# Longer assumed latencies between DVE or ACT and the small products, in an instruction order made by a planner

## The chip, the cores and the metric

The kernel runs on one core of one Trainium2 chip. The metric is the device time of one execution in microseconds (us), as a median of several executions; lower is better. The engines are called as in the profile: PE (matrix products), DVE (vector), ACT (scalar), POOL (GpSimd) and SP (issues of DMA transfers).

## What is computed

Two residual layers on x of 2048 positions by 1024 channels, all in float32. The first layer's mixer is a gated linear recurrence, the second a gated delta rule with 8 heads of 128 by 128. Cut to what matters here:

```
h = rmsnorm(x) * (1 + scale_c) + shift_c                      # c: conditioning
# layer 0: RG-LRU
xb, zg = split(h @ in_w);  xb = causal_conv4(xb) + b
r, i   = sigmoid(blockdiag(gate_w) @ xb + gate_b)             # 8 blocks of 128 x 128
a      = exp(-8 * r * softplus(-lam))
y_t    = a_t * y_{t-1} + sqrt(1 - a_t^2) * i_t * xb_t
x      = x + gate_c * ((y * silu(zg)) @ out_w)
# layer 1: gated delta rule, per head
q, k, v = silu(causal_conv4(h @ in_w));  q, k normalized
S_t = a_t S_{t-1} + beta_t k_t (v_t - a_t S_{t-1}^T k_t)^T;   o_t = S_t^T q_t
x   = x + gate_c * ((rmsnorm(o) * silu(z)) @ out_w)
return rmsnorm(x) * final_g
```

## The kernel before: five stages, and a planner that writes the order

**Stages.** PE's long work is in four projections of 128x512 products on f32r operands, all issued at L670: each float32 operand is split into a high and a low part, and each product is made of three (high by high, high by low, low by high), 24 products for one panel of 128 channels and one tile of 512 positions. In the order in which they run: the input projection of layer 0 for the first and the second half of the sequence (32 jobs of 24 products each half), its output projection, the input projection of layer 1 for the first and the second half (64 jobs each), its output projection. I call these products the main products.

**Small products between them.** In layer 0 each tile of a channel block passes from PE to ACT (L730, a copy), POOL (L744, the first tap), DVE (L718, three taps), ACT (L768, the high part `xh`) and DVE (L771, the low part `xl`), and then returns to PE for the two gates: six products `pg` at L777, of which the second reads `xl`. In layer 1 the tiles of k, q and v come from DVE at L978. From k, PE makes transposes `pk` (L1090) and the Gram blocks `pkk` (L1125), from q and k the blocks `pqk` (L1210). The inverse of a triangular matrix is built for each head: 62 short instructions on DVE for its 32x32 blocks (L1245, L1248, with `blk`, `tblk` and `ttmp`), and three levels that merge blocks with four groups of small products, `px` (L1287), `pr` (L1299, L1302), `px` (L1316) and `pr` (L1326), each of which waits for ACT or DVE to bring back the one before. Then the recurrence of the head runs over 8 chunks of 128 positions for each half of the sequence. One chunk is a closed chain:

- PE `pp` (L1365, L1366): state by k and by q
- DVE `zt` (L1374)
- PE `py` (L1382)
- ACT `yt` (L1388)
- PE `pS` (L1394, L1395)
- DVE: the new state (L1407), which the next `pp` reads.

**The order.** Nothing is ordered on the chip except by each engine's own queue and by semaphores. The queues are written by a planner (class `Weave`) that runs when the program is built. Each piece of work is a generator; it says which engine it wants and for how long, and optionally what latency follows until a reader on another engine can start. The planner always takes the thread that can start first:

```
            else:
                self.free[w[0]] = t + w[1]
                th.t = t + w[1] + (w[2] if len(w) > 2 else self.LAG[w[0]])
```

Here `w[0]` is the engine, `w[1]` the assumed duration, and `w[2]` the assumed latency; without it the latency is `LAG`, 0.3 for DVE and ACT. A reader can thus not be placed before the assumed duration and latency are over, and the planner fills PE with main products meanwhile. Buffers are counted slots: a thread that asks for one of them stops until an earlier holder gives it back. The ones that matter here are those of layer 1: `kt` has 6 and `qt` 5 tiles (`KTN, QTN`), `ac`, `atn`, `kd` and `vn` have 4, and each head uses two of each for a half of the sequence. A job of main products for k or q asks for its `kt` or `qt` tile before its first product, and the recurrence gives one back after the `pp` of every fourth chunk. The thread that issues main products works through its jobs one after the other, so a job that waits for a tile holds up all main products.

Of the kernel before, what the change touches and what calls it, by code (L numbers as in the profile page):

```python
# [31 lines left out]
BLK = 2  # L32
KTN, QTN = 6, 5
EPS = 1e-6

# [103 lines left out]
def trunk_kernel(ctx, tc, x, c, ada_w, ada_b, ada_c, norm_c, final_g, w1, cw1, cb1, gate_w, gate_b, lam, ow1,  # L139
                 w2, wab, cw2, a_log, dt_bias, onorm, ow2, out):  # L140
    nc = tc.nc
    act, dve, pool, pe, sp = nc.scalar, nc.vector, nc.gpsimd, nc.tensor, nc.sync
# [616 lines left out]
    def gates_thread(u, n, i):  # L759
# [8 lines left out]
        act.copy(xh, xf)  # L768
        yield "dve", EV
        xl = tile_([P, TC], "xr", "xl", F32R)  # L770
# [181 lines left out]
    def conv2_thread(u, kind, h, i, pt, mtok, rtok):  # L952
# [21 lines left out]
        if kind == "v":  # L974
            rtok = yield slots["vt"]
        yield "dve", EV
        r = tile_([P, TC], kind + "t", kind + "t")
# [282 lines left out]
    def levels_thread(u, h):  # L1260
# [15 lines left out]
        for b in range(3):  # L1276
            for i in range(NTC):
                yield "dve", 0.2, 0.0 if b < 2 or i == 0 else 0.27
                o = 32 * (b % 2)
                dve.transpose(out=tf[32 * b:32 * b + 32, i, :, o:o + 32],  # L1280
                              in_=acs[i][32 * b:32 * b + 32, :, 32 * b:32 * b + 32])
# [8 lines left out]
        act.activation(tf[32:64, :, :, 0:32], px[32:64], AF.Copy, scale=-1.0)  # L1290
        yield "dve", 0.33
        dve.tensor_scalar(tf[96:128, :, :, 0:32], px[96:128], -1.0, None, ALU.mult)
# [15 lines left out]
        for i, a in ((0, 0), (1, 0), (1, 64)):  # L1308
            yield "dve", 0.2, 0.27 if a else 0.0
            dve.tensor_copy(out=acs[i][a:a + 32, :, a + 32:a + 64], in_=pr[a:a + 32, 0, i])  # L1310
# [7 lines left out]
        act.activation(tf[64:128, 0], px[64:128, 0], AF.Copy, scale=-1.0)  # L1318
        yield "dve", 0.33
        dve.tensor_scalar(tf[64:128, 1], px[64:128, 1], -1.0, None, ALU.mult)  # L1320
# [19 lines left out]
    def recurrence_thread(u, h):  # L1340
# [4 lines left out]
        for i in range(NTC):  # L1345
# [7 lines left out]
            for b in range(TB):  # L1353
# [16 lines left out]
                if not first:  # L1370
                    ztok = yield slots["zt"]
                    yield "dve", 0.27
                    zt = tile_([P, P], "zt", "zt")
                    dve.scalar_tensor_tensor(zt, pp[:, 0, :], eg[:, 0, m, h:h + 1], vn[:, b, :], ALU.mult,  # L1374
                                             ALU.subtract)
                    hold.done()
# [8 lines left out]
                ytok = yield slots["yt"]  # L1385
                yield "act", 0.16
                yt = tile_([P, P], "yt", "yt")
# [13 lines left out]
                if last:  # L1401
                    return
                yield "dve", 0.27
                if first:
# [334 lines left out]
```

## Time and profile before

| | |
|---|---|
| median of three runs | 1983.85 us (1979.78 to 1991.28) |
| time of the profiled execution | 1989.06 us |
| its span, first to last instruction | 1987.3 us, granted clock of PE 0.981 |
| busy | PE 1869.0, DVE 1500.0, ACT 1025.1, POOL 811.3 us |

The profile gives, for each instruction, its engine, line, start and duration, and for an engine's idle time the instruction elsewhere that ended it. A duration of PE overlaps with that of the next product, so PE's pace is read from the distance of two starts and not from the mean duration. Lines of a view of waits read: engine and line that waited, `<-` what it waited for, us in total, times, longest.

### The profile page before, as it was taken

To read this page: it belongs to the slowest core of one execution; us is meant where nothing else is said; L and a number is where in the kernel's file an instruction comes from. 1 tells how busy PE (TensorE), PEld (TensorE's weight loads), DVE (VectorE), ACT (ScalarE), POOL (GpSimd) and SP (SyncE) were. 2 spreads that over 40 slices of the span, in tenths; PEclk is the share of its full clock that TensorE was granted. 3 is DMA by queue.
4 is the path that set the end of the run, shared out by engine and by line. 5 is a ranking of instruction groups with operands and counts; after the bars stand their busy time and mean duration, and the time that the engine had idled before them with its cause. 6 is when DMAs were issued, how large, how long until landed. Compare 5 with 4: busy or idle time off the path is not lost.

```text
span 1987.3 us, 31679 instructions
## 1 busy us (share of the span) xinstructions
PE 1869.0 (94%) x10408; PEld 1520.6 (77%) x10408; DVE 1500.0 (75%) x3176; ACT 1025.1 (52%) x2453; POOL 811.3 (41%) x1439
## 2 busy tenths in 40 slices
PE   6998889999999999999998989999999999999998
PEld 3776667787787777777777777788888888878887
DVE  6788798887644566888888897778777778877654
ACT  3655567666411225455555655555655556655321
POOL 4555664444200146555555553364343335511101
PEclk9999999999999999999999999999999999999999
DMA  8355655654578724546764447455455445577751
GB/s 333 97 159 160 220 169 171 199 170 156 172 199 206 223 63 127 136 111 160 177 161 126 107 115 187 135 125 146 114 129 142 120 127 128 142 208 233 224 185 64
DMA packets 506957, 314.33 MB, mean 158 GB/s; under 512 B 370724, under 2 KB 438564, under 8 KB 506792
## 3 DMA queue, kind: packets, MB, share of 16 engines
q1 hardware_dynamic: 506792, 312.31, 55.5%
q8 instruction: 82, 1.34, 0.3%
q14 instruction: 83, 0.68, 0.1%
HBM read 211.54 MB, written 100.67 MB: 157 GB/s over the span
## 4 chain that ended last, share of the span: by engine, by line
PE 50%; DVE 20%; DMA 10%; POOL 6%; issue 5%; ACT 5%; SPq 4%; DVEq 0%; POOLq 0%; ACTq 0%
PE mm L670 25%; PE mmo L670 12%; DVE xf L718 5%; DVE tblk L1248 2%; DVE ttmp L1245 2%; PE pg L777 2%; SPq L515 1%; DMA raw<-in_w 1%; DMA pq<-q_d 1%; DVE acc L415 1%; PE pp L1365 1%; PE py L1382 1%; DMA ada<-in_ada_w 1%; PE pS L1394 1%; PE pS L1395 1%
## 5 line engine op out<-in xcount | busy, mean ns | idle before, releaser
L718 DVE SCALAR_TENSOR_TENSOR xf<-xe,cw_s,xf 128x512 f32<-128x512 f32 x384 | 327.8, 855 | 54.9 <-POOL xf L961 32.0
L652 POOL TENSOR_TENSOR wlo<-raw,whi 128x1024 fp32r<-128x1024 f32 x48 | 122.3, 2548 | 81.0 <-ACT whi L646 67.9
L733 POOL COPY carry<-xe 128x4 f32<-128x4 f32 x128 | 36.8, 287 | 249.3 <-ACT xe L730 248.4
L1245 DVE TENSOR_TENSOR ttmp<-blk,tblk 128x60 f32<-128x60 f32 (+24 forms) x496 | 121.9, 246 | 21.0 <-DMA blk<-blk_d 11.0
L1248 DVE TENSOR_TENSOR tblk<-tblk,ttmp 128x60 f32<-128x60 f32 (+24 forms) x496 | 127.3, 257 | 10.1
L646 ACT CAST whi<-raw 128x1024 fp32r<-128x1024 f32 x96 | 100.3, 1045 | 52.8 <-DMA raw<-in_w 43.5
L730 ACT COPY xe<-mm 128x512 f32<-128x512 f32 x128 | 74.1, 580 | 78.6 <-PE mm L670 77.8
L670 PE MATMUL mmo<-oh,yh 128*128 128x512 f32 x256 | 102.2, 399 | 7.3 <-DVE xr L925 6.2
L670 PE MATMUL mm<-hh_('in2', 0)_5430,wlo 128*128 128x512 f32 x256 | 105.1, 411 | 0.0
L670 PE MATMUL mm<-hl_('in2', 0)_5431,whi 128*128 128x512 f32 x256 | 105.1, 410 | 0.0
L670 PE MATMUL mm<-hl_('in2', 1)_12333,whi 128*128 128x512 f32 x256 | 104.8, 409 | 0.0
L670 PE MATMUL mm<-hh_('in2', 0)_5430,whi 128*128 128x512 f32 x256 | 104.4, 408 | 0.0
L670 PE MATMUL mm<-hh_('in2', 1)_12332,wlo 128*128 128x512 f32 x256 | 104.3, 408 | 0.0
L670 PE MATMUL mm<-hh_('in2', 1)_12512,wlo 128*128 128x512 f32 x256 | 104.1, 407 | 0.0
L670 PE MATMUL mm<-hl_('in2', 0)_5208,whi 128*128 128x512 f32 x256 | 103.6, 405 | 0.0
L670 PE MATMUL mm<-hh_('in2', 0)_5207,whi 128*128 128x512 f32 x256 | 103.4, 404 | 0.2 <-ACT xe L730 0.2
L670 PE MATMUL mm<-hh_('in2', 0)_5207,wlo 128*128 128x512 f32 x256 | 103.5, 404 | 0.0
L670 PE MATMUL mm<-hh_('in2', 1)_12512,whi 128*128 128x512 f32 x256 | 103.5, 404 | 0.0
L670 PE MATMUL mm<-hl_('in2', 1)_12513,whi 128*128 128x512 f32 x256 | 103.2, 403 | 0.0
L670 PE MATMUL mm<-hh_('in2', 1)_12332,whi 128*128 128x512 f32 x256 | 103.1, 403 | 0.0
L670 PE MATMUL mmo<-oh,yl 128*128 128x512 f32 x256 | 101.7, 397 | 1.3 <-DVE yl L899 1.3
L670 PE MATMUL mmo<-oh,oh 128*128 128x512 f32 (+1 forms) x264 | 102.1, 387 | 0.0
(325 smaller groups left out, 5857.8 us busy)
## 6 DMA issues: line engine op xcount, KB each, us to landing
raw<-in_w SPq DMA_DIRECT2D x96, 512.0 KB, 4.3
araw<-in_ada_w SPq DMA_DIRECT2D x32, 512.0 KB, 4.6
xt<-x_d SPq DMA_DIRECT2D x32, 512.0 KB, 5.1
xt_d<-xb SPq DMA_DIRECT2D x192, 64.0 KB, 2.2
xk<-xt_d SPq DMA_DIRECT2D x24, 512.0 KB, 6.1
xt<-in_x SPq DMA_DIRECT2D x16, 512.0 KB, 5.1
ada<-in_ada_w SPq DMA_DIRECT2D x16, 512.0 KB, 9.0
y_d<-tz SPq DMA_DIRECT2D x32, 256.0 KB, 3.0
```

Source lines behind the costliest of these rows:

```text
L415: dve.scalar_tensor_tensor(acc, raw[:, k, :], ck, acc, ALU.mult, ALU.add)
L515: sp.dma_start(out=dst[c_], in_=tb[32 * c_:32 * c_ + 32])
L646: act.copy(hi, raw)
L652: pool.tensor_tensor(lo, raw, f(hi), ALU.subtract)
L670: pe.matmul(pt, lhsT=lhs[a][:, k, :], rhs=rhs[b][:, k, :], start=(k == 0 and n == 0), stop=(k == KT - 1 and n == 2))
L718: dve.scalar_tensor_tensor(xf, xe[:, 1 + j:1 + j + TC], wc[:, j:j + 1], xf, ALU.mult, ALU.add)
L730: act.copy(xe[:, 4:4 + TC], pt)
L733: pool.tensor_copy(out=carry, in_=xe[:, TC:TC + 4])
L777: pe.matmul(pg, lhsT=a[:, g, :], rhs=b, start=(q == 0), stop=(q == 2))
L1245: dve.tensor_tensor(tmp, blk[:, j, j + 1:32].unsqueeze(2).to_broadcast([P, r, c_]), t[:, j, 0:c_].unsqueeze(1).to_broadcast([P, r, c_]), A ...
L1248: dve.tensor_tensor(t[:, j + 1:32, 0:c_], t[:, j + 1:32, 0:c_], tmp, ALU.subtract)
L1365: pe.matmul(pp[:, 0, :], lhsT=kc, rhs=S_, start=True, stop=True)
```

## The change

A constant `SLACK = 0.8` is added, and nine yields of the planner get a latency from it: eight get 0.8 in place of 0.3 or 0.27, and the one behind `xl` gets 1.6 in place of 0.3. No instruction is added, removed or given another shape; only the order in which the planner puts them differs, on all five engines. The assumed durations stay as they are.

```
+SLACK = 0.8
...
@@ gates_thread: xl, for the gate products pg
-        yield "dve", EV
+        yield "dve", EV, SLACK + 0.8
@@ conv2_thread: kt, qt, vt
-        yield "dve", EV
+        yield "dve", EV, SLACK
@@ levels_thread: four places, of this form
-                yield "dve", 0.2, 0.0 if b < 2 or i == 0 else 0.27
+                yield "dve", 0.2, 0.0 if b < 2 or i == 0 else SLACK
...
-        yield "dve", 0.33
+        yield "dve", 0.33, SLACK
@@ recurrence_thread: zt, yt, the new state
-                    yield "dve", 0.27
+                    yield "dve", 0.27, SLACK
...
-                yield "act", 0.16
+                yield "act", 0.16, SLACK
...
-                yield "dve", 0.27
+                yield "dve", 0.27, SLACK
```

Three places of the order follow, before and after. In the changed kernel every line number is one higher, and the rows' numbers are their places in the engine's queue.

**A chunk of the recurrence** in the third head of the second half of the sequence, on PE, from `py` to `pS`; first before:

```order
5667 L1382 MATMUL py<-zt,ac 128x128
5668 L670 MATMUL mm<-hh_('in2', 1)_12332,wlo 128x512
5669 L670 MATMUL mm<-hh_('in2', 1)_12332,whi 128x512
5670 L670 MATMUL mm<-hl_('in2', 1)_12333,whi 128x512
5671 L670 MATMUL mm<-hh_('in2', 1)_12332,wlo 128x512
5672 L1394 MATMUL pS<-yt,kd 128x128
5673 L1395 MATMUL pS<-yt,at 128x128
```

and the same chunk after:

```order
5715 L1383 MATMUL py<-zt,ac 128x128
5716 L671 MATMUL mm<-hl_('in2', 1)_12378,whi 128x512
5717 L671 MATMUL mm<-hh_('in2', 1)_12377,wlo 128x512
5718 L671 MATMUL mm<-hh_('in2', 1)_12377,whi 128x512
5719 L671 MATMUL mm<-hl_('in2', 1)_12378,whi 128x512
5720 L671 MATMUL mm<-hh_('in2', 1)_12377,wlo 128x512
5721 L1080 MATMUL pd<-eh,lstrict 128x256
5722 L1080 MATMUL pd<-el,lstrict 128x256
5723 L1395 MATMUL pS<-yt,kd 128x128
5724 L1396 MATMUL pS<-yt,at 128x128
```

Where four main products stood between `py` and the `pS` that reads ACT's `yt`, five and two others stand now.

**The fifth head of the first half**, on PE, from the last level of its inverse (`pr`) on; before:

```order
4000 L1326 MATMUL pr_10287<-ac,tf 64x64 x8
4001 L670 MATMUL mm<-hh_('in2', 0)_5430,whi 128x512
4002 L670 MATMUL mm<-hl_('in2', 0)_5431,whi 128x512
4003 L670 MATMUL mm<-hh_('in2', 0)_5430,wlo 128x512
4004 L670 MATMUL mm<-hh_('in2', 0)_5430,whi 128x512
4005 L1382 MATMUL py<-vn,ac 128x128
4006 L670 MATMUL mm<-hl_('in2', 0)_5431,whi 128x512
4007 L670 MATMUL mm<-hh_('in2', 0)_5430,wlo 128x512
4008 L670 MATMUL mm<-hh_('in2', 0)_5430,whi 128x512
4009 L670 MATMUL mm<-hl_('in2', 0)_5431,whi 128x512
4010 L1394 MATMUL pS<-yt,kd 128x128
4011 L1395 MATMUL pS<-yt,at 128x128
```

and after:

```order
4146 L1327 MATMUL pr_10707<-ac,tf 64x64 x8
4147 L1383 MATMUL py<-vn,ac 128x128
4148 L1395 MATMUL pS<-yt,kd 128x128
4149 L1396 MATMUL pS<-yt,at 128x128
4150 L1366 MATMUL pp<-state_116,kt 128x128
4151 L1367 MATMUL pp<-state_116,qt 128x128
4152 L1383 MATMUL py<-zt,ac 128x128
4153 L1395 MATMUL pS<-yt,kd 128x128
4154 L1396 MATMUL pS<-yt,at 128x128
4155 L1366 MATMUL pp<-state_116,kt 128x128
4156 L1367 MATMUL pp<-state_116,qt 128x128
4157 L1383 MATMUL py<-zt,ac 128x128
```

After, no main product stands between the small ones, from row 4128 (the first `pr`) to row 4161 (the fourth chunk's `pp`, after which a `qt` tile is given back): the next job of main products is the sixth of the seventh head, which asks for that tile, and it starts at row 4162.

**DVE's queue ahead of `xl`**, in the first half of layer 0, at the first tile of the last channel block; before:

```order
264 L718 SCALAR_TENSOR_TENSOR xf_2244<-xe_2223,cw_s,xf_2244 128x512 x2
265 L804 TENSOR_TENSOR tg<-tg 128x512
266 L808 SCALAR_TENSOR_TENSOR tg<-th,tg 128x512
267 L415 SCALAR_TENSOR_TENSOR acc<-araw,c_col,acc 128x512 x2
268 L804 TENSOR_TENSOR tg<-tg 128x512
269 L573 CAST hh_('in1', 1)_2271<-h 128x512
270 L808 SCALAR_TENSOR_TENSOR tg<-th,hcar,tg 128x512
271 L579 TENSOR_TENSOR hl_('in1', 1)_2272<-h,hh_('in1', 1)_2271 128x512
272 L573 CAST hh_('in1', 1)_2271<-h 128x512
273 L771 TENSOR_TENSOR xl<-xf_2244,xh 128x512
```

and after:

```order
267 L809 SCALAR_TENSOR_TENSOR tg<-th,tg 128x512
268 L719 SCALAR_TENSOR_TENSOR xf_2267<-xe_2252,cw_s,xf_2267 128x512 x3
269 L805 TENSOR_TENSOR tg<-tg 128x512
270 L809 SCALAR_TENSOR_TENSOR tg<-th,hcar,tg 128x512
271 L772 TENSOR_TENSOR xl<-xf_2267,xh 128x512
```

Nine instructions stood between the tile's last taps and its `xl`; two stand there now. In the queue of PE the gate products of this tile stand 48 main products behind the tile's own job before, and 41 after.

More of the change, by code (lines that the diff above doesn't have):

```diff
@@ L1308, in levels_thread @@
         for i, a in ((0, 0), (1, 0), (1, 64)):
-            yield "dve", 0.2, 0.27 if a else 0.0
+            yield "dve", 0.2, SLACK if a else 0.0
             dve.tensor_copy(out=acs[i][a:a + 32, :, a + 32:a + 64], in_=pr[a:a + 32, 0, i])
@@ L1318, in levels_thread @@
         act.activation(tf[64:128, 0], px[64:128, 0], AF.Copy, scale=-1.0)
-        yield "dve", 0.33
+        yield "dve", 0.33, SLACK
         dve.tensor_scalar(tf[64:128, 1], px[64:128, 1], -1.0, None, ALU.mult)
```

## The prediction

> **What bounds the kernel now.** I read the page first, then the busy time by stage, then who PE waits for, and last single chains on the timeline. From the page, the span, the busy line, and PE and DVE in 40 slices:
>
> ```profile
> span 1987.3 us, 31679 instructions
> PE 1869.0 (94%) x10408; PEld 1520.6 (77%) x10408; DVE 1500.0 (75%) x3176; ACT 1025.1 (52%) x2453; POOL 811.3 (41%) x1439
> ...
> PE   6998889999999999999998989999999999999998
> ...
> DVE  6788798887644566888888897778777778877654
> ```
>
> PE is the bound, but not everywhere: it has gaps where DVE is at 8 of 10. The stages, with the columns PE, PEld, DVE, ACT, POOL, granted clock, DMA share and GB/s (first and second half of layer 0; then of layer 1; then the last projection):
>
> ```profile
> 38.00:292.00 254.00, 223.95 (x904) 176.03 (x903) 211.85 (x251) 149.37 (x213) 151.03 (x148) 0.93 0.55 167
> 292.00:507.00 215.00, 208.16 (x900) 167.69 (x899) 177.89 (x221) 147.20 (x191) 97.02 (x107) 0.98 0.52 169
> ...
> 701.00:1261.00 560.00, 519.11 (x3289) 423.85 (x3288) 456.91 (x1170) 297.75 (x895) 291.89 (x555) 0.99 0.53 135
> 1261.00:1793.00 532.00, 525.05 (x3526) 437.42 (x3525) 414.71 (x1188) 310.26 (x940) 211.10 (x517) 1.00 0.53 139
> 1793.00:1988.00 195.00, 187.22 (x949) 156.41 (x947) 113.00 (x150) 58.08 (x135) 23.07 (x58) 0.99 0.56 173
> ```
>
> PE idles 30 us in the first half of layer 0, 41 in the first half of layer 1, and only 7 in each of the two second halves. So the change can win in two stages. What PE waited for there, among the readers that the change moves:
>
> ```profile
> PE pg L777 <- DVE xl L771: 22.8, 13, 5.2
> ...
> PE pp L1365 <- DVE state L1407: 8.1, 8, 2.0
> ...
> PE py L1382 <- DVE zt L1374: 5.4, 5, 1.6
> PE pS L1394 <- ACT yt L1388: 4.9, 9, 1.6
> ...
> PE pqk L1210 <- DVE qt L978: 3.9, 3, 1.4
> ...
> PE px L1287 <- DVE tf L1280: 3.5, 4, 1.9
> PE pp L1365 <- DVE tblk L1248: 3.4, 2, 1.8
> PE pk L1090 <- DVE kt L978: 3.0, 4, 1.1
> PE pk L1090 <- DVE ttmp L1245: 2.9, 2, 2.7
> ```
>
> Together 57.9 us in 50 waits: 22.8 in layer 0 and 35.1 in layer 1. That is all that later places could save directly.
>
> **What a link of the recurrence takes.** Where nothing else is in DVE's way, one chunk on the timeline:
>
> ```profile
> 1807.82 0.39 PE L1365 MATMUL pp<-state,kt 128*128 128x128 f32 x2
> 1808.47 0.35 DVE L1374 SCALAR_TENSOR_TENSOR zt<-pp,eg,vn 128x128 f32<-128x128 f32 x1 [0.82 <-PE pp L1366]
> 1809.18 0.38 PE L1382 MATMUL py<-zt,ac 128*128 128x128 f32 x2
> 1809.60 0.28 ACT L1388 ACTIVATE yt<-py 128x128 f32<-128x128 f32 x1 [0.38 <-PE py L1382]
> 1810.34 0.38 PE L1394 MATMUL pS<-yt,kd 128*128 128x128 f32 x2
> 1810.98 0.35 DVE L1407 SCALAR_TENSOR_TENSOR state<-state,eg,pS 128x128 f32<-128x128 f32 x1 [0.39 <-PE pS L1395]
> ```
>
> From the start of `pp` to the end of `zt` 1.00 us, of `py` to `yt` 0.70, of `pS` to the state 0.99. And where taps stand ahead of `zt` in DVE's queue:
>
> ```profile
> 846.39 0.47 PE L1365 MATMUL pp<-state,kt 128*128 128x128 f32 x2
> 846.70 0.39 PE L1366 MATMUL pp<-state,qt 128*128 128x128 f32 x2
> ...
> 847.16 0.39 PE L670 MATMUL mm<-hl_('in2', 0)_5208,whi 128*128 128x512 f32 x1
> 847.39 0.39 PE L670 MATMUL mm<-hh_('in2', 0)_5207,wlo 128*128 128x512 f32 x1
> ...
> 848.62 0.74 DVE L718 SCALAR_TENSOR_TENSOR xf<-xe,cw_s,xf 128x512 f32<-128x512 f32 x1
> ...
> 849.28 0.34 DVE L1374 SCALAR_TENSOR_TENSOR zt<-pp,eg,vn 128x128 f32<-128x128 f32 x1
> ...
> 849.67 0.49 PE L1382 MATMUL py<-zt,ac 128*128 128x128 f32 x2 [1.43 <-DVE zt L1374]
> 849.92 0.47 PE L670 MATMUL mm<-hh_('in2', 0)_5207,wlo 128*128 128x512 f32 x1
> ...
> 850.23 0.39 PE L670 MATMUL mm<-hh_('in2', 0)_5207,whi 128*128 128x512 f32 x1
> ```
>
> A main product follows another after 0.23 us. Five of them and the pair of `pp` covered the typical link, not this one, and PE stood for 1.43 us. PE goes on 0.05 us after `zt` ends. The first main product after a small one costs 0.31.
>
> **Term A, the gate products: 6 us gained.** Alone, the 1.3 us of added latency put `pg` six main products later (6 x 0.23 = 1.4 us). Taken off each of 13 waits, with the small ones counted whole, this saves at most about 13 of the 22.8. But the order does not keep the rest still. At the longest wait the gate products stand 41 main products behind their tile's job where they stood 48, so the wait gains no time from PE; it is DVE's queue that got lighter there, by seven instructions. At five of the other places the rows' work of L415 comes ahead of `xl`. A row of L415 costs
>
> ```profile
> L415 DVE SCALAR_TENSOR_TENSOR acc<-araw,c_col,acc 128x512 f32<-128x512 f32 x56 | 50.7, 905 | 5.9 <-DMA araw<-in_ada_w 5.5
> ```
>
> 0.9 us, and six more of them stand ahead; if half of that doesn't fit into DVE's idle time (42 us in this stage), 3 us are lost. So the waits are redistributed, and I take 4 us gained, nearer to the loss than to the 13. The longest wait shows a second price:
>
> ```profile
> 280.00:290.00 10.00, 6.67 (x20) 5.04 (x21) 8.82 (x13) 7.26 (x10) 6.98 (x7) 0.66 0.65 207
> ...
> 283.32 0.80 PE L777 MATMUL pg<-xl,gh 128*128 128x512 f32 x1 [5.16 <-DVE xl L771]
> ...
> 283.92 0.63 PE L777 MATMUL pg<-xh,gl 128*128 128x512 f32 x1
> ```
>
> After 5.16 us of standing, the next product starts 0.60 us later and not 0.23, and the granted clock in these 10 us is 0.66. With 0.93 over the stage of 254 us, the clock costs at most 18 us there, and less by the part in which PE stands anyway. I add 2 us for one or two of the waits that fall under the size that triggers it. The Trainium skill, page "TensorE: Matmul & The Clock Gate", section "What's actually happening", has PE at half rate after at least one idle window of about 3.4 us, and at full rate again after a busy one. By that rule only waits above 3.4 us pay, and the 2 us would be nothing unless one of those falls below it; the rows here agree on the slower clock after 5.16 us, and do not show the threshold.
>
> **Term B, layer 1's waits: 22 us gained.** Counted over all chunks, the median PE work in a link grows from 1.5 to 2.1 us (`pp` to `py`), 1.2 to 1.7 (`py` to `pS`) and 1.4 to 2.1 (`pS` to `pp`), at 0.23 us a main product. So about 0.55 us come off each of 37 waits, 20 us if none is shorter. Beyond that, in the fourth to eighth head of the first half DVE has less queued ahead of k and q at the same main product, because the inverses come later; this takes more off `pk`, `pqk` and `pp`. I take 22, between 8 (waits that only move to the next link) and all 35.
>
> **Term C, new stretches without main products: 17 us lost.** The longer chains give back `qt` and `kt` later, and five is too few: in the first half of layer 1 the order has places where main products stop until a recurrence has caught up. The worst is in the fifth head, shown above: eight links of the recurrence and three of the levels with nothing between them. An uncovered link costs its latency less PE's own work in it: 1.00 + 0.05 - 0.44, 0.70 + 0.05 - 0.22, 0.99 + 0.05 - 0.44, about 0.6 each. Over this place and three smaller ones there are 17 links with too little cover; counted one by one they lack 8.3 us, and five links of levels (three here, two in the seventh head) another 3: 11 us at least. More, where DVE has other work queued between: in the fifth head's stretch 31 instructions of the next head's inverse stand among the chain's, at
>
> ```profile
> L1245 DVE TENSOR_TENSOR ttmp<-blk,tblk 128x60 f32<-128x60 f32 (+24 forms) x496 | 121.9, 246 | 21.0 <-DMA blk<-blk_d 11.0 <-issue 0.6
> L1248 DVE TENSOR_TENSOR tblk<-tblk,ttmp 128x60 f32<-128x60 f32 (+24 forms) x496 | 127.3, 257 | 10.1
> ```
>
> 0.25 us, 7.8 us, and with a tap, two transposes and the chain's own steps some 16 us, of which PE fills 3.6: 12.5 us instead of 7. So 12.5 here, 4 at the other links, 1 in the seventh head. At the upper end a tap (0.74) also stands before each of the nine other links, 7, and the clock falls twice, at 2.5 (10 x 0.34, less what PE stands): 29. Behind the waiting products stands the next job of main products, and so its copy on ACT and taps on POOL and DVE; DVE has the inverse to do meanwhile. POOL and SP keep their work (POOL is busy 292 of 560 us), so nothing is set for the moves in their queues.
>
> **Term D, switches: 2 us gained.** Main products are interrupted 559 times and not 587; 28 x (0.31 - 0.23).
>
> **Term E, the end: nothing.** The last head's last `pS` stands 150 main products (34 us) later, deep in the last projection. Its ninth block, the first that needs all heads, comes 88 products, 20 us, behind it. PE idles 7 us in this stage now. If the chain from `pS` to that block takes over 20 us, up to 10 us are lost.
>
> Sum: -6 - 22 + 17 - 2 = -13 us on the profiled execution (span 1987.3, its time 1989.06, 5 above the median). On the median of 1983.85 that is **1971 us**.
>
> **The rivals.**
>
> *The waits only move.* DVE is busy for 212 of 254 and 457 of 560 us, in the two stages that can win. If its queue sets their pace, PE meets the same DVE work a little later, the waits come back at the next reader, and the stretches of C are where DVE catches up: A 0, B -8, C +8, D -2, 1982 us. For it: at the longest wait the products do not even stand later, so the change does not do there what it says. Against it: DVE is idle for 42 and 103 us.
>
> *The planner stalls its own main products (slower).* Place: the first half of layer 1, third to eighth head. Price: C at its upper end of 29, with A at 3 lost, B at 8 gained and D: 29 + 3 - 8 - 2 = +22, 2006 us. It decides from the point where C exceeds A, B and D by 10. For it: five `qt` tiles, and chains that are half as long again. Against it: the stretch is one long one, and DVE works during it.
>
> *All waits go.* A 13 plus 6 of clock, B 33, C 11, D 2: -43, 1941 us. Against it: the longest waits, 5.2, 2.7 and 2.0, exceed what is added.
>
> *The end is exposed*, term E: 1981 us.
>
> **How the numbers follow.** One can tell a measurement of this kernel from no change at about 0.5%, 10 us: below 1974 is faster, above 1994 slower. Chances: forecast 0.42 (of which 0.34 below 1974), all waits go 0.10, waits only move 0.22, stalls 0.20, the end 0.06 (half of it slower). Faster 0.44, same 0.33, slower 0.23. The range of 8 in 10 ends a little inside the two extreme cases and leaves out about half of each, 0.15: 1945 to 1999. The forecast's own is 1960 to 1982.
>
> **What would show it.** In the profile after: `pg <- xl` at 17 to 19 us; `pp`, `py`, `pS`, `pk` and `pqk` together near 13; new waits of `py`, `pS` and `pp` bunched within some 16 us in the fifth head of the first half, where PE's digit falls; the second halves and the last stage unchanged or 2 to 4 us shorter. Wrong, if the first half of layer 1 is longer than its 560 us by 10, if the bunch costs under 5, or if PE waits in the last stage.

## The result, and the profile after

The changed kernel takes 2014.95 us (median of four runs, 2010.2 to 2017.79) against 1986.34 us of the kernel before on the same chip: a ratio of 1.0154, 95% interval 1.0134 to 1.0174, slower by 1.5%. The profiled execution took 2017.79 us, 28.7 more than that of before. In the changed kernel every line number is one higher (L671 for the main products of L670). From its page, the span, the busy line, and PE, DVE and PE's granted clock in 40 slices:

```profile
span 2016.1 us, 31683 instructions
PE 1878.8 (93%) x10408; PEld 1540.0 (76%) x10408; DVE 1496.4 (74%) x3176; ACT 1020.1 (51%) x2453; POOL 805.7 (40%) x1439
...
PE   6998888999999999999898798999999999999998
...
DVE  6788988887644567869868767778778778877654
...
PEclk9999999999999999999898799899999999999999
```

PE makes the same 10408 products and is busy for 9.8 us longer (1869.0 before); DVE, ACT and POOL are busy for no longer. So about a third of the 29 us is time in which PE works more slowly, and the rest, some 19 us, is time in which it stands. A slice is 50.4 us. In slices 20, 22 and 23, and again in 25 and 26, PE or its clock drops where PE before stood at 9 or, once, at 8: from 958 us to 1310. The stages confirm it (columns PE, PEld, DVE, ACT, POOL, granted clock, DMA share, GB/s; the two halves of layer 0, the two of layer 1, the last projection):

```profile
38.00:291.00 253.00, 221.38 (x910) 174.01 (x909) 214.96 (x252) 144.41 (x208) 145.40 (x146) 0.94 0.56 170
291.00:511.00 220.00, 208.58 (x896) 167.50 (x896) 179.48 (x222) 150.23 (x196) 92.24 (x109) 0.98 0.50 166
...
698.00:1285.00 587.00, 531.04 (x3232) 437.68 (x3232) 440.37 (x1148) 290.04 (x866) 288.40 (x549) 0.94 0.49 127
1285.00:1814.00 529.00, 522.66 (x3515) 441.03 (x3514) 414.74 (x1176) 310.50 (x948) 218.12 (x519) 1.00 0.53 139
1814.00:2016.00 202.00, 193.59 (x1017) 161.35 (x1015) 120.61 (x184) 62.67 (x156) 24.18 (x61) 0.99 0.56 171
```

The first half of layer 1 takes 587 us and not 560; the other stages differ by at most 7 us, in both directions. Its clock is 0.94 and was 0.99: if the loss is time at half clock, that is (1 - 0.94) x 587 / 0.5 = 70 us at half clock, where it was (1 - 0.99) x 560 / 0.5 = 11. How the difference builds up is read from the main products alone, since there are 6168 of them in both kernels and in the same order. The start of the n-th, from the timeline, in us:

| main product | before | after | difference |
|---|---|---|---|
| 2304 (first of layer 1) | 701.0 | 697.8 | -3.2 |
| 3000 | 941.9 | 931.7 | -10.2 |
| 3480 | 1128.7 | 1112.5 | -16.2 |
| 3540 | 1145.4 | 1155.9 | +10.5 |
| 3780 | 1242.8 | 1249.2 | +6.4 |
| 3840 (first of the second half) | 1261.1 | 1285.4 | +24.3 |
| 4080 | 1349.3 | 1377.6 | +28.3 |
| 6120 | 1974.3 | 2003.1 | +28.8 |

The changed kernel is ahead for more than half of its time. (At 3480 it is ahead by more than it has gained, because 190 small products still stand behind.) It loses most in two steps, 26.7 us at 3480 to 3540 and 17.9 at 3780 to 3840. Each step is a stretch in which no main product runs. The first is the fifth head's; its first and last rows, and one chunk inside, from the timeline:

```profile
1125.76 0.39 PE L671 MATMUL mm<-hh_('in2', 0)_5207,wlo 128*128 128x512 f32 x1
...
1140.50 0.80 PE L1366 MATMUL pp<-state,kt 128*128 128x128 f32 x2 [0.38 <-DVE state L1406]
...
1141.80 0.34 DVE L1375 SCALAR_TENSOR_TENSOR zt<-pp,eg,vn 128x128 f32<-128x128 f32 x1
...
1142.20 0.80 PE L1383 MATMUL py<-zt,ac 128*128 128x128 f32 x2 [0.48 <-DVE zt L1375]
...
1143.03 0.28 ACT L1389 ACTIVATE yt<-py 128x128 f32<-128x128 f32 x1 [0.49 <-PE py L1383]
...
1143.36 0.79 PE L1395 MATMUL pS<-yt,kd 128*128 128x128 f32 x2 [0.37 <-ACT yt L1389]
...
1144.65 0.18 DVE L1246 TENSOR_TENSOR ttmp<-blk,tblk 128x24 f32<-128x24 f32 x1
1144.75 0.34 DVE L1408 SCALAR_TENSOR_TENSOR state<-state,eg,pS 128x128 f32<-128x128 f32 x1
...
1145.15 0.80 PE L1366 MATMUL pp<-state,kt 128*128 128x128 f32 x2 [0.57 <-DVE state L1408]
...
1150.52 0.77 PE L671 MATMUL mm<-hh_('in2', 0)_5430,whi 128*128 128x512 f32 x1
```

From 1125.76 to 1150.52 there is no main product: 24.8 us. A chunk, from `pp` to the next `pp`, takes 4.65 us. Two things make it slow at once. A small product of 0.39 us now takes 0.80, so PE is at half clock (the stretch's granted clock is 0.60); the waits of PE in the stretch add up to only 9.7 of its 24.8 us. And the state waits behind the inverse of the next head: `pS` starts at 1143.36, and at 1144.65 DVE still runs a `ttmp`. What DVE has in its queue there, in groups of its lines from 1126 to 1150:

```profile
L1246 DVE TENSOR_TENSOR ttmp<-blk,tblk 128x60 f32<-128x60 f32 (+18 forms) x21 | 6.5, 310 | 0.4
L719 DVE SCALAR_TENSOR_TENSOR xf<-xe,cw_s,xf 128x512 f32<-128x512 f32 x7 | 5.2, 743 | 0.0
L1249 DVE TENSOR_TENSOR tblk<-tblk,ttmp 128x60 f32<-128x60 f32 (+18 forms) x21 | 4.4, 207 | 0.4
```

42 instructions of the inverse, and seven taps of main products that ran before the stretch: 16.1 us of the 20.27 us that DVE is busy in these 24. Last, what PE waited for, in the whole span:

```profile
PE pg L778 <- DVE xl L772: 13.2, 9, 5.6
PE adapt L427 <- DVE acc L416: 8.8, 3, 4.3
PE pp L1366 <- DVE state L1408: 7.6, 6, 3.2
PE pqk L1211 <- DVE tblk L1249: 6.6, 3, 3.2
...
PE pS L1395 <- ACT yt L1389: 5.9, 7, 2.0
...
PE mm L671 <- DVE tz L756: 5.4, 3, 3.6
...
PE adapt L284 <- DVE acc L416: 4.9, 2, 3.0
```

and before, of the same readers in layer 0:

```profile
PE adapt L426 <- DVE acc L415: 3.9, 2, 2.8
...
PE adapt L283 <- DVE acc L415: 3.5, 3, 1.7
...
PE mm L670 <- DVE tz L755: 0.4, 1, 0.4
```

The gate products' wait has fallen from 22.8 to 13.2 us, more than forecast. But PE now stands in front of `adapt` for 8.8 and 4.9 us (3.9 and 3.5 before), and for 5.4 (0.4 before) in front of a main product whose tile `tz` of L756 has not been emptied.

### The profile page after: what moved, and what is told of

Same layout as the page of the kernel before. It is cut to its first block, busy times and chain, and to the rows that moved or that the text cites. A ratio compares the mean times of both kernels' runs of the same rounds, so it can differ in the third digit from the quotient of the medians.

```text
span 2016.1 us, 31683 instructions
## 1 busy us (share of the span) xinstructions
PE 1878.8 (93%) x10408; PEld 1540.0 (76%) x10408; DVE 1496.4 (74%) x3176; ACT 1020.1 (51%) x2453; POOL 805.7 (40%) x1439
## 4 chain that ended last, share of the span: by engine, by line
PE 54%; DVE 18%; DMA 9%; POOL 6%; issue 5%; ACT 4%; SPq 3%; DVEq 0%; POOLq 0%; ACTq 0%
PE mm L671 27%; PE mmo L671 14%; DVE xf L719 5%; DVE ttmp L1246 2%; DVE tblk L1249 2%; PE py L1383 1%; PE pg L778 1%; PE pS L1395 1%; PE pkk L1126 1%; PE pp L1366 1%; PE pS L1396 1%; PE pp L1367 1%; DMA ada<-in_ada_w 1%; DMA xk<-xt_d 1%; PE pqk L1211 1%
## 5 line engine op out<-in xcount | busy, mean ns | idle before, releaser
L719 DVE SCALAR_TENSOR_TENSOR xf<-xe,cw_s,xf 128x512 f32<-128x512 f32 x384 | 319.5, 833 | 46.8 <-POOL xf L962 22.8
L1246 DVE TENSOR_TENSOR ttmp<-blk,tblk 128x60 f32<-128x60 f32 (+24 forms) x496 | 126.7, 256 | 26.8 <-POOL tblk L1240 6.1
L1249 DVE TENSOR_TENSOR tblk<-tblk,ttmp 128x60 f32<-128x60 f32 (+24 forms) x496 | 120.9, 244 | 10.4 <-POOL tblk L1240 0.5
L671 PE MATMUL mm<-hh_('in2', 0)_5430,whi 128*128 128x512 f32 x256 | 106.8, 417 | 5.1 <-DVE tz L990 3.2
L671 PE MATMUL mmo<-oh,yh 128*128 128x512 f32 x256 | 101.3, 396 | 6.3 <-DVE xr L926 6.3
L671 PE MATMUL mm<-hh_('in2', 1)_12377,whi 128*128 128x512 f32 x256 | 104.3, 407 | 2.5 <-DVE tz L990 2.4
L671 PE MATMUL mm<-hh_('in2', 0)_5430,wlo 128*128 128x512 f32 x256 | 106.0, 414 | 0.0
L671 PE MATMUL mm<-hl_('in2', 0)_5431,whi 128*128 128x512 f32 x256 | 105.5, 412 | 0.0
L671 PE MATMUL mm<-hh_('in2', 1)_12077,whi 128*128 128x512 f32 x256 | 104.9, 410 | 0.0
L671 PE MATMUL mm<-hh_('in2', 0)_5207,whi 128*128 128x512 f32 x256 | 104.7, 409 | 0.0
L671 PE MATMUL mm<-hl_('in2', 1)_12378,whi 128*128 128x512 f32 x256 | 103.9, 406 | 0.0
L671 PE MATMUL mm<-hl_('in2', 0)_5208,whi 128*128 128x512 f32 x256 | 103.7, 405 | 0.0
L671 PE MATMUL mm<-hh_('in2', 1)_12377,wlo 128*128 128x512 f32 x256 | 103.6, 405 | 0.0
L671 PE MATMUL mm<-hh_('in2', 1)_12077,wlo 128*128 128x512 f32 x256 | 103.5, 404 | 0.0
L671 PE MATMUL mmo<-oh,oh 128*128 128x512 f32 (+1 forms) x264 | 102.2, 387 | 1.4 <-DVE xt L1576 1.4
L671 PE MATMUL mm<-hh_('in2', 0)_5207,wlo 128*128 128x512 f32 x256 | 103.3, 404 | 0.0
L671 PE MATMUL mmo<-oh,ol 128*128 128x512 f32 (+1 forms) x264 | 103.2, 391 | 0.0
L671 PE MATMUL mm<-hl_('in2', 1)_12078,whi 128*128 128x512 f32 x256 | 102.7, 401 | 0.0
```

The costliest lines, as they stand in the source:

```text
L671: pe.matmul(pt, lhsT=lhs[a][:, k, :], rhs=rhs[b][:, k, :], start=(k == 0 and n == 0), stop=(k == KT - 1 and n == 2))
L719: dve.scalar_tensor_tensor(xf, xe[:, 1 + j:1 + j + TC], wc[:, j:j + 1], xf, ALU.mult, ALU.add)
L1246: dve.tensor_tensor(tmp, blk[:, j, j + 1:32].unsqueeze(2).to_broadcast([P, r, c_]), t[:, j, 0:c_].unsqueeze(1).to_broadcast([P, r, c_]), A ...
L1249: dve.tensor_tensor(t[:, j + 1:32, 0:c_], t[:, j + 1:32, 0:c_], tmp, ALU.subtract)
```

## The experiments

All kernels were run against the kernel before on the same chip, three rounds each (the last one five); an edit of the change is shown against the changed kernel or, where part of it is kept, against the kernel before. Their line numbers are those of before. Beside the time stands, for each, the sum of its stretches: distances between neighbouring main products of layer 1 that exceed 6 us, read from the timeline.

| kernel | ratio to before | interval | stretches, us |
|---|---|---|---|
| before | 1 | | none |
| after | 1.0154 | 1.0134 to 1.0174 | 10.1, 24.8, 16.0, 6.2: 57 |
| gates alone | 1.0007 | 0.9989 to 1.0024 | none |
| layer 1 alone | 1.0144 | 1.0122 to 1.0165 | 9.3, 24.4, 15.1, 6.2: 55 |
| recurrence alone | 1.0139 | 1.0115 to 1.0164 | 6.1, 21.6, 7.9, 20.5: 56 |
| k, q, v and levels alone | 1.0024 | 1.0009 to 1.0038 | none |
| filler products | 1.0172 | 1.0152 to 1.0192 | 10.1, 25.2, 16.3, 6.2: 58 |
| second half alone | 0.9988 | 0.9972 to 1.0004 | none |
| 0.5 everywhere | 0.9975 | 0.9958 to 0.9991 | none |
| six `qt` tiles | 1.0171 | 1.0145 to 1.0198 | 9.6, 11.7, 20.3, 17.3, 6.2: 65 |
| no sixth inverse | 1.0142 | 1.0111 to 1.0173 | 10.1, 20.8, 17.3, 6.2: 54 |
| 0.60 everywhere | 1.0008 | 0.9991 to 1.0025 | 13.5 |
| 0.65 everywhere | 1.0118 | 1.0071 to 1.0165 | 10.2, 10.2, 6.8, 6.9: 34 |
| 0.6 and 0.8 | 0.9972 | 0.9954 to 0.9990 | 11.4 |
| filler, no inverse | 1.0134 | 1.0109 to 1.0160 | 10.1, 21.2, 16.5, 6.2: 54 |
| 0.5 and 0.8 | 1.0007 | 0.9993 to 1.0022 | none |

**Which part of the change.** Four runs keep one part each. The gate products alone:

```
-        yield "dve", EV            # gates_thread, behind xl
+        yield "dve", EV, 1.6
```

> Only the latency behind xl (1.6) is kept; layer 1's order is that of before. Theory of the stretches (the loss lies where main products stop in the first half of layer 1, because the recurrence holds kt and qt longer): within 5 us of before, most likely 3 faster, since the changed kernel's two stages of layer 0 and its output projection end 3 us earlier. Rival (later places cost everywhere, since DVE's queue gets a worse order): 5 us or more slower.

No change, 1985.37 us. The waits of `pg` fall as in the changed kernel, and others take their place:

```profile
PE pg L777 <- DVE xl L771: 11.8, 8, 5.6
...
PE adapt L426 <- DVE acc L415: 7.5, 3, 4.0
...
PE mm L670 <- DVE tz L755: 5.5, 3, 3.5
```

11.0 us less at `pg`, and 3.6 and 5.1 more at the next two readers of DVE's queue. In layer 0 the waits only move: all waits of PE up to main product 1536, where the input projection of layer 0 ends, add up to 38.5 us in this run and to 36.7 before.

Everything but the gate products:

```
-        yield "dve", EV, SLACK + 0.8    # gates_thread
+        yield "dve", EV, 0.3
```

> The latency behind xl is back at 0.3; all of layer 1's are 0.8. Theory of the stretches: 28 to 34 us slower than before, with the first half of layer 1 at 585 us in place of 560. Rival (the loss is spread): under 20 us slower.

2012.69 us: the loss is all in layer 1. Then only the three yields of the recurrence (`zt`, `yt` and the state), and only those of the levels and of `kt`, `qt` and `vt`:

```
-                    yield "dve", 0.27           # zt; likewise the state
+                    yield "dve", 0.27, 0.8
-                yield "act", 0.16               # yt
+                yield "act", 0.16, 0.8
```

> 0.8 behind zt, yt and the state alone. The order has 17 links of the recurrence with too little cover, as many as the whole change. Theory of the stretches: 20 to 35 us slower than before, the loss in the first half of layer 1. Rival (the levels' and the convolution's latencies carry part of it): under 15 us slower.

```
-        yield "dve", EV                         # kt, qt, vt
+        yield "dve", EV, 0.8
-        yield "dve", 0.33                       # levels, two places; two more of 0.27
+        yield "dve", 0.33, 0.8
```

> 0.8 behind kt, qt, vt and in the levels, the old latencies in the recurrence and behind xl. The order has no link of the recurrence with too little cover. Theory of the stretches: 4 to 12 us faster than before, from the waits of pk, pqk and px (11 us of waits for DVE before). Rival (later places cost everywhere): 5 us or more slower.

The recurrence alone makes the whole loss (2011.57 us) and the same stretch at main product 3528. The other part has no stretch, but not the gain of 4 to 12 us either: 1988.22 us, by its interval a little slower than before. Its stages (both halves of layer 1, and the last projection):

```profile
697.60:1248.40 550.80, 517.38 (x3284) 423.77 (x3283) 455.19 (x1167) 296.01 (x891) 293.19 (x553) 0.99 0.54 138
1248.50:1787.30 538.80, 525.12 (x3497) 438.37 (x3496) 412.14 (x1185) 309.70 (x941) 211.94 (x517) 0.99 0.52 135
1787.40:1990.60 203.20, 193.22 (x983) 161.03 (x982) 114.77 (x155) 58.52 (x138) 23.76 (x59) 0.97 0.54 168
```

The first half is 9 us shorter than the 560 of before, and the second half 7 and the last stage 8 us longer than their 532 and 195. What is saved in one stage comes back in the next two: PE's waits fall from 40.5 to 33.0 us in the first half and grow from 6.6 to 16.2 in the second.

**Whether the stretches are the loss.** The longer latencies only in the second half of layer 1, where the order has no stretch; and 0.5 us at all places, where it has none either. (In the first of these runs the gate products' latency is 0.3, and in the first half two of the levels' are 0.27 where the kernel before has 0.3.)

```
-                    yield "dve", 0.27, SLACK     # and so at the other seven places of layer 1
+                    yield "dve", 0.27, (SLACK if u else 0.3)
```

> The longer latencies only in the second half of layer 1; the old ones in the first half and for the gate products. Theory (the loss is the places of the first half where the main products stop until a recurrence has given back its qt tiles; the order of this kernel has one link of the recurrence with too little cover, as before): first half of layer 1 near 560 us, time within 6 us of before, 1977 to 1989. Rival (later places for the small products cost PE time everywhere, by longer chains, a fuller queue of DVE or an end that comes too late): second half and last projection together 10 to 15 us longer, time near 1997.

```
-SLACK = 0.8
+SLACK = 0.5
```

> The same change at all its places, with 0.5 us in place of 0.8 (1.3 for the gate products). Theory (a threshold: five qt tiles suffice for chains of this length, so the order has 2 links of the recurrence with too little cover in place of 17): first half of layer 1 within 8 us of the 560 of before, no stretch of over 10 us at half clock there, time 1975 to 1990. Rival (in proportion to the slack): about 0.5 of 0.8 less the old 0.3, so two fifths of the loss of 30 us, 1995, with the first half of layer 1 some 11 us longer.

1981.39 and 1979.93 us: no loss in either. Links that are longer by 0.2 us, or in the second half by the change's whole 0.5 us, cost nothing while main products remain between them. Then two values a twentieth of a microsecond apart. In the order with 0.60 no link of the recurrence has less PE work than its latency in the first half; in that with 0.65 there are 16:

```
-SLACK = 0.8
+SLACK = 0.6      # and 0.65
```

> The change at all its places with 0.6 us in place of 0.8 (1.4 for the gate products). The order has no link of the recurrence with too little cover in the first half of layer 1. Theory (a threshold, with stretches or without): first half of layer 1 at 545 to 558 us, time 1973 to 1988. Rival (the loss grows in proportion from 0.3 to 0.8): 18 us above before, 2003.

> The change at all its places with 0.65 us (1.45 for the gate products), a twentieth of a microsecond more than in the run with 0.6. The order now has 16 links with too little cover, five after main product 3528 and three after 3576, where those of the changed kernel lie, and eight around 3850. Theory (a threshold): a step of over 10 us at main product 3528 that the run with 0.6 does not have, first half of layer 1 at 565 to 590, time 10 to 25 us above that with 0.6. Rival (in proportion): within 4 us of it.

1985.96 and 2008.82 us: a step of 22.9 us for 0.05 us, so the loss has a threshold and does not grow in proportion. The step at 3528 is there with 0.65, 10.2 us, and not with 0.60. Two of the expectations failed in detail: 0.60 has a stretch of 13.5 us at product 3072 that the count of links had not shown (three groups of small products of one head's levels, and then a main product that waits 4.0 us for DVE's `tz`), and with 0.65 the first half itself, 560.3 us from product 2304 to 3840, is no longer than before (560.2; 554.8 with 0.60), since three of the four stretches, 23.9 us, end at product 3858 or behind it, in the first jobs of the second half. Nor does the whole step come from stretches: between the two profiled executions, 22.7 us apart, 6.0 us lie ahead of product 2304, 5.5 in the first half, 16.0 between 3840 and 4080, and 4.8 are won back behind that. The 6.0 in layer 0 are as much as single executions differ there (see term A below). Over the table, kernels without a stretch lie between 1980 and 1988 us, those with 11 to 14 us between 1982 and 1986, that with 34 at 2009, and those with 54 to 65 between 2009 and 2020.

**What makes main products stop.** The forecast named the five `qt` tiles. With six:

```
-KTN, QTN = 6, 5
+KTN, QTN = 6, 6
...
-        "zt": 2, "t2": 2, "yt": 2
+        "zt": 1, "t2": 2, "yt": 1
```

> The changed kernel with six qt tiles in place of five; to make room zt and yt have one tile each in place of two, and the scratch of the decays shares another tile's place. Theory (the main products stop because qt is given back late): the order has 13 links with too little cover in place of 17, now where kt binds, and none in the fifth head's old place; the stretch of 24 us is gone and a shorter one stands a little later; time 5 to 15 us under the changed kernel's, 2000 to 2010. Rival (qt is not what holds the main products back, or the single zt and yt tiles cost as much): time within 4 us of the changed kernel's or above it.

2018.49 us, no better. The stretch left main product 3528, where the job of the seventh head's second `qt` tile begins, and came back one and two jobs later, at 3552 (11.7 us) and 3576 (20.3), with the eighth head's two `kt` tiles. So the tiles do decide where the main products stop, and one tile of one kind only shifts the place. That holds for the stretches at 3192 and 3528, where a job for a `qt` tile begins. The stretch at 3792 (16.0 us, and 17.3 with six `qt` tiles) is another: the job that begins there is one of z, which asks for neither tile, but, as every job does, for one of the two tiles `mm` that main products write to. The rival (the single `zt` and `yt` cost as much) is not excluded by this run. More tiles of both kinds were not tried; there was no room for them.

**Why the worst stretch is 24.8 us long.** Two suspects, the half clock and DVE's queue, one taken away in each of two runs. Filler products into the same tiles, overwritten by the real ones, keep PE busy:

```
+    fill = lambda u, h, i, o, a, n=3: [pe.matmul(o, lhsT=a, rhs=upper, start=True, stop=True)
+                                       for _ in range(n if (u, h, i) == (0, 4, 0) else 0)]
...
+                fill(u, h, i, py, rm[:, b, :])      # likewise ahead of pp, pS, pr, px2 and pr2
                 pe.matmul(py, lhsT=rm[:, b, :], rhs=zt, start=True, stop=True)
```

> The changed kernel, with extra small products into the tiles of pr, px, py, pp and pS of the fifth head of the first half of layer 1 (three or four ahead of each real product, into the same tile, which the real one then overwrites), so that PE is not idle while the chain of that head runs. Theory (the chain's latency costs some 16 us there as forecast, and the half clock lengthens it to 24): PE keeps a granted clock above 0.9 in that stretch, the stretch from its first pr to the next main product falls from 24 us to 15 to 18, and the time is 6 to 10 us under the changed kernel's, near 2006. Rival (the latency of DVE and ACT alone makes the 24 us, the clock only shows that PE is idle): the stretch stays at 22 to 25 us and the time within 3 us of the changed kernel's.

```
-            dve.tensor_tensor(tmp, blk[:, j, j + 1:32] ...
+            if (u, h) != (0, 5): dve.tensor_tensor(tmp, blk[:, j, j + 1:32] ...
```

> The changed kernel without the 62 subtraction steps on DVE of one inverse, that of the sixth head of the first half of layer 1 (left out, so that head's numbers differ); every other instruction in the same order on every engine. 42 of the 62, 10.9 us of DVE, run while the main products stand still for the fifth head's chain. Theory (DVE's queue, not the clock, sets the length of that stretch: DVE is busy for 20 of its 24 us): the stretch falls from 24 us to 12 to 16, the first half of layer 1 from 587 us by 8 to 12, the time to 2003 to 2007. Rival (the chain's own latency sets it, DVE's other work fits in between): the stretch stays above 20 us and the time within 4 us of the changed kernel's.

Neither theory held; by time and stretch the second run came out as its rival had it, and the first nearly so. With fillers the time is 2019.85 us and the stretch 25.2, although the clock came back in the recurrence. (In the levels ahead of it the groups of fillers take 1.1, 1.2 and 2.0 us themselves, so the length of the whole stretch does not tell what the clock alone is worth.) One chunk of the recurrence, from `pp` to `pp`:

```profile
1143.82 0.39 PE L1365 MATMUL pp<-state,kt 128*128 128x128 f32 x2
...
1147.96 0.34 DVE L1407 SCALAR_TENSOR_TENSOR state<-state,eg,pS 128x128 f32<-128x128 f32 x1
...
1148.35 0.49 PE L1365 MATMUL pp<-state,kt 128*128 128x128 f32 x2 [0.51 <-DVE state L1407]
```

Products of 0.39 us again, so full clock, and still 4.53 us: the state comes when DVE's queue lets it. Without the inverse the time is 2013.57 us and the stretch 20.8; a chunk there:

```profile
1138.11 0.80 PE L1365 MATMUL pp<-state,kt 128*128 128x128 f32 x2 [0.38 <-DVE state L1405]
...
1142.20 0.35 DVE L1407 SCALAR_TENSOR_TENSOR state<-state,eg,pS 128x128 f32<-128x128 f32 x1 [2.48 <-PE pS L1395]
...
1142.60 0.79 PE L1365 MATMUL pp<-state,kt 128*128 128x128 f32 x2 [0.44 <-DVE state L1407]
```

Here DVE stood for 2.48 us before the state, so nothing was queued ahead of it, and still 4.49 us: products of 0.80 us, half clock. Either suspect alone gives the same chunk. That called for both edits in one kernel:

```
+    fill = ...                                  # as above, with n=2
...
+            if (u, h) != (0, 5): dve.tensor_tensor( ...
```

> The two edits together: filler products in the fifth head's chain (two ahead of each real product of the recurrence, four in the levels) and the sixth head's inverse left out on DVE. Each alone left a chunk of that chain, from pp to pp, at 4.5 us against 4.65 in the changed kernel: at half clock with DVE free 4.49, at full clock with DVE's queue 4.53. Theory (either of the two is enough, so only taking both away shows): a chunk takes 2.9 to 3.4 us, the chain from its first py to the next main product 8 to 10 us and not 12 to 13, and the time is 4 to 8 us under the changed kernel's. Rival (something third, in the chain itself, sets the 4.5 us): a chunk stays above 4.2 us and the time within 3 us of the changed kernel's.

```profile
1138.01 0.63 PE L1365 MATMUL pp<-state,kt 128*128 128x128 f32 x2
...
1141.32 0.49 PE L1365 MATMUL pp<-state,kt 128*128 128x128 f32 x2
...
1144.48 0.49 PE L1365 MATMUL pp<-state,kt 128*128 128x128 f32 x2
```

3.31 and 3.16 us a chunk, as the theory had it. (Some 0.2 us of the difference to the run with fillers alone are the third filler: `pS` starts 0.65 us after `yt` with three, 0.43 with two.) The recurrence's part of the stretch, from its first `py` to the next main product, fell from 12.8 us (1137.73 to 1150.52 in the changed kernel; 12.6 without the inverse alone) to 9.9, or 10.9 with the fillers ahead of that `py`. The stretch as a whole is 21.2 us, because in the levels ahead of it the fillers stand on the path themselves (groups of eight passes, 1.1 us each). The time is 2009.46 us; the ratios' intervals of this and the changed kernel overlap (1.0109 to 1.0160 and 1.0134 to 1.0174), so the times don't show the 4 to 8 us. In the two profiled executions main product 3840 starts 6.8 us earlier than in the changed kernel; 2.0 of these were there ahead of the stretch, and 3.5 come in it (24.8 to 21.2).

**Whether the gain can be had.** Two kernels take the slack that leaves no long stretch in the first half, and 0.8 in the second half, where it lost nothing:

```
-                    yield "dve", 0.27, SLACK     # and so at the other seven places of layer 1
+                    yield "dve", 0.27, (SLACK if u else 0.6)
```

> The longer latencies where the runs so far show a gain: 0.6 us in the first half of layer 1, 0.8 in its second half, 1.6 in all for the gate products. Theory (the gain up to the first stretch, some 12 us, stays when there is no stretch, and the second half is neutral or 3 us shorter): 1967 to 1976, below both kernels. Rival (waits that are saved in one stage come back in the next): 1978 to 1986.

```
-                    yield "dve", 0.27, SLACK     # the same places; 1.3 for the gate products
+                    yield "dve", 0.27, (SLACK if u else 0.5)
```

> 0.5 us in the first half of layer 1, 0.8 in its second half, 1.3 in all for the gate products. Of the run with 0.5 everywhere, main product 3840 (end of the first half) was reached 13.8 us earlier than before and the gain was lost after product 5400; with 0.8 in the second half nothing was lost there. Theory (no stretch without main products, so the saved waits stay): the time is 10 to 16 us under before, 1968 to 1974. Rival (saved waits come back in later stages): 1978 to 1984, as with 0.5 everywhere.

1981.85 and 1986.39 us; neither reaches what was expected. The first is 0.28% under the kernel before by an interval that ends at 0.9990, as the run with 0.5 everywhere is 0.25% under it; both are less than the 0.5% that was taken as the limit. The second shows where a lead goes. Main product 3840 starts 18.2 us ahead of before (10.0 of these were there at 2304, ahead of layer 1), 4080 still 10.5, and 6000 only 1.8. 5.9 us of that are lost at one place in the last projection, in waits of PE at 1807 and 1809 us that the kernel before does not have:

```profile
PE mmo L670 <- ACT oh L1527: 4.3, 1, 4.3
PE mmo L670 <- DVE ol L1530: 1.6, 1, 1.6
```

The operands of the last projection (`oh`, `ol`) come from ACT and DVE, and ACT stood for 1.00 us for DVE before this `oh`: DVE's queue still held work of the last heads. PE arrives earlier, and they don't.

## Why the prediction was wrong

The forecast was 1971 us, faster; the result is 2014.95, outside the range, and the way is the rival in which the planner stalls its own main products, at a price above the 2006 us worked out for it. On the profiled execution the terms come out, from the table of main products, as follows.

- **Term A** (6 us gained): the runs show no gain. The direct part was more than forecast (9.6 us off `pg`'s wait for `xl`, where 4 were taken), but it all came back: up to main product 1536 `pg` waits for 16.7 us over all that it waited for (22.3 before), `adapt` for 13.7 (7.3) and the main products for 9.9 (4.5). There the changed kernel is 3.4 us behind, and the run of the gate products alone 4.1. That it is 3.2 ahead at 2304 says nothing: four kernels whose order in all of layer 0 is that of before (layer 1 alone, recurrence alone, k, q, v and levels alone, second half alone) are 3.3 to 6.5 us ahead there, so single executions differ by that much. Whether the clock gained cannot be told: the first half of layer 0 has 0.94 after 0.93, and the hundredth is as much as the 2 us forecast.
- **Term B** (22 us gained): about half of it. From main product 2304 to 3000, ahead of the first stretch, it is 7.0. `pp`, `py`, `pS`, `pk` and `pqk` together, which were to come to near 13 us, waited for 33.8 (9.7, 4.9, 5.9, 3.9 and 9.4, over all that they waited for), as against 35.7 before (12.4, 7.0, 5.1, 7.3 and 3.9). But 10.5 of the 33.8 lie in the stretches and belong to term C. Outside them the first four fell from 31.8 to 13.9, nearly as forecast, and `pqk` rose from 3.9 to 9.4: 12.4 us came off the five. The step that failed is "this takes more off `pk`, `pqk` and `pp`": `pqk` no longer waits for its `qt` but for DVE's inverse (`tblk`, 6.6 us). The run with k, q, v and levels alone shows the same further on: 9 us saved in the first half, 7 and 8 lost behind it. So the rival "the waits only move" was right in part, and its price for this term (8) is nearer than the 22.
- **Term C** (17 us lost, 29 at most): 34.5 between main products 3000 and 3840. This is the term that turned the sign, and its size is the step of the forecast that failed most. For the longest stretch the place and the cause were right (the fifth head, eight links of the recurrence and three of levels, held up by the return of tiles); its price was not: "some 16 us" for it, where it took 24.8. Three steps went wrong. First, DVE's queue: 31 instructions of the inverse and one tap were counted into the stretch, 42 and seven taps were there, because DVE was behind with the taps of earlier main products when PE arrived; a list of the order shows who stands between two instructions, but not what an engine still owes. (With that inverse left out the stretch is still 20.8 us.) Second, the clock: two falls were priced at 2.5 us each, and in the upper end alone; the first half of layer 1 has some 59 us more at half clock than before by the estimate above (70 and 11), and in this stretch the half clock is by itself enough to keep a chunk at 4.5 us with DVE free. Third, "1 in the seventh head": the levels there made a stretch of 16.0 us. Its rows:

```profile
1257.99 0.80 ACT L566 ACTIVATE h<-xk,cond 128x512 f32<-128x512 f32 x1
1258.81 0.37 ACT L1291 ACTIVATE tf<-px 32x256 f32<-32x256 f32 x1
...
1259.23 0.26 PE L1300 MATMUL pr<-ac,tf 32*32 32x32 f32 x1 [3.27 <-ACT tf L1291]
...
1267.68 0.79 PE L671 MATMUL mm<-hh_('in2', 0)_5430,whi 128*128 128x512 f32 x1 [3.16 <-DVE tz L990]
```

  The first `tf` of the levels stands behind the second half's `h` in ACT's queue and is 3.27 us late for PE, and at the end the main product itself waits 3.16 us for its tile to be emptied by DVE. Counting two links of levels at their bare latency left out both queues. And no `kt` or `qt` tile holds up the job that starts here.
- **Term D** (2 us gained): too small to be seen in any run.
- **Term E** (0, at most 10 lost): 0.5 us between main products 4080 and 6120; right in sum. The last stage is 7 us longer and the second half of layer 1 is 3 shorter, since 134 more of the last heads' small products stand behind main product 5400; PE waits for 1.4 us in the last projection, where it did not wait before. The exposed end came in a kernel that reaches the last stage earlier, that with 0.5 and 0.8.

By position the sum is -3.2 - 7.0 + 34.5 at product 3840, and 4.5 more behind it: 28.8, which is the 28.7 us between the two profiled executions. The working of the threshold from which the slower rival decides (C above A, B and D by 10) was right. What was said against it, that the stretch is one long one and that DVE works during it, was no argument, since DVE's work stands on the chain's own path. Two of the signs that were to show the forecast wrong are there: the first half of layer 1 is 27 us longer, and PE waits in the last stage.

## What to carry to other kernels

A planner's assumed latency is a lever with a threshold: in this kernel values up to 0.60 us changed the time by a quarter of a per cent at most, and a twentieth of a microsecond more cost 1.2%. So count the places where the order leaves the long work's engine nothing but a dependent chain, and count levels of an inverse as well as links of a recurrence. Price such a place by its chain at the reduced clock and by everything that the other engines still owe on arrival, the larger of the two, and not by bare latencies; and when two causes run side by side, only an experiment without both shows either. A saved wait is not yet a gain: the engine that caused it has as much to do as before, and here much of what was saved came back at a later reader.

## What the runs showed of the hardware

PE's clock stayed at half through a stretch in which PE kept working. Two windows of the changed kernel, the stretch and its second part:

```profile
1126.00:1150.00 24.00, 14.33 (x108) 11.17 (x108) 20.27 (x70) 8.12 (x26) 2.32 (x5) 0.60 0.32 72
1137.00:1150.00 13.00, 8.85 (x27) 6.50 (x28) 9.53 (x41) 4.65 (x19) 0.00 (x0) 0.50 0.36 71
```

In the 13 us from 1137 on PE is busy for 8.85, its waits are 1.42 us at most, and the granted clock is 0.50 throughout. With filler products in the 25.2 us of the same stretch PE is busy for 21.7 and the clock is 0.80:

```profile
1127.50:1152.70 25.20, 21.72 (x190) 19.88 (x189) 20.51 (x70) 6.40 (x17) 2.55 (x5) 0.80 0.29 66
```

The Trainium skill, page "TensorE: Matmul & The Clock Gate", section "What's actually happening", has PE at half rate after an idle window of about 3.4 us and at full rate after a busy one. The longest wait in this stretch was 2.49 us, so here the clock fell and stayed down without a single wait of that length. The runs do not show at which share of busy time it returns.
